# Four gate-up units side by side, modulation sums by transposes, other down groups, tiles moved by 32 bytes: a two-layer hybrid step on one core

## The chip, the cores and the metric

The kernel runs on one core of a Trainium2 chip. The metric is the time of one execution on the device in microseconds (us). Engines carry the profile's names: PE is TensorE's matmul, PEld its weight load, DVE is VectorE, ACT ScalarE, POOL GpSimd, SP SyncE, which issues the DMAs.

## The reference

One inference step of two layers with width 1024 over 1024 latent tokens and 256 prompt tokens. Cut to what matters here:

```
mod_p = silu(c_ctx) @ w_mod[l] + b_mod[l]          # six vectors of 1024 for prompt tokens
mod_s = silu(c) @ w_mod[l] + b_mod[l]              # the same for latent tokens
...
hp = modulate(rms_norm(xp, norm_mix[l]), sh1_p, sc1_p)
hs = modulate(rms_norm(xs, norm_mix[l]), sh1_s, sc1_s)
... # layer 0: neighbourhood attention and pooling; layer 1: windowed attention
xp = xp + g1_p * op
xs = xs + g1_s * os_
hp = modulate(rms_norm(xp, norm_ffn[l]), sh2_p, sc2_p)
hs = modulate(rms_norm(xs, norm_ffn[l]), sh2_s, sc2_s)
xp = xp + g2_p * swiglu(hp, w_gate_up[l], w_down[l])
xs = xs + g2_s * swiglu(hs, w_gate_up[l], w_down[l])
...
y_prompt = rms_norm(xp, norm_final)
y_sample = rms_norm(xs, norm_final)
```

`swiglu` is (silu(h @ gate) * (h @ up)) @ down, with 2816 hidden columns (22 units of 128).

## The kernel before, in words

**Numbers in parts.** Every large product is a sum of three matmuls: operands are split into a high and a low part, and high weights meet both parts of the activations, low weights the high part (`dense_k`, L302 to L308; `prod`, L851 to L858; `mix`, L967 to L976). ScalarE makes the high part, VectorE or GpSimd the low one.

**Blocks.** Tokens come in three blocks: ti = 0 and 1 are latent tokens (512 each), ti = 2 is the prompt (256). A matmul has 512 or 256 columns.

**Weights.** `Weights` (L220) keeps a fixed list of units in the order in which TensorE takes them. A unit is loaded, in some cases summed by GpSimd (L270 to L274), split by ScalarE (L279) and VectorE (L281) into one of four `whl` buffers. `done(i)` starts the split of unit i + 4.

**FFN.** `out_proj` (L794) ends a mixer: two groups of four output rows, each over ti = 0, 1, 2; L809 adds the result to the residual x, the second group feeds the norm. Then `ffn` (L835) runs 22 units. For the latent blocks a unit is seven products of 12 matmuls in Strassen's manner (Q11, Q21, T2, T1, T3, Q22, T4), which need sums of the two latent blocks as operands (T1 to T4) and sums of gate and up weights (units G, A, B, U of the weight list). For the prompt it is a gate and an up product of 24 matmuls with 256 columns. `front(i)` issues Q11 and Q21, `prompt_gate(i)` the prompt's gate, `back(i)` the rest. At the start the order is front(0), front(1), both prompt gates, back(0), back(1).

**Operands of the FFN.** `norm_parts` (L471) returns tasks that turn x into operands: `scaled` (L478, reads the norm factor in PSUM), `high` (L481), `low` (L484), and for the latent blocks `first` to `fourth` (L511 to L532), whose low parts GpSimd makes (L496). They stand in a background list; `bg.step(n)` runs up to n of them as the matmuls are recorded, and `bg.need(key)` all that carry a key. Every engine keeps the recorded order.

**Modulation ahead of time.** `Mod` (L346) computes modulation vectors for later use on VectorE: for each of 20 blocks j of 512 columns, 8 steps of two accumulations (L375, L377) into two tiles, one per condition; then `sum` (L384): matmuls with ones over the 128 partitions and a copy by ScalarE (L389); then `finish` (L391): four transposes (L394) and `mod_done` (L320). That is 10 steps per block. `md.step()` calls stand in the input projection of layer 0 (60 of them), in its output projection and in its FFN; `md.all()` runs what is left at the end of a stage. Layer 1 has none.

**Down.** The hidden units are spilled to DRAM (`hd`) and come back in groups of 4, 4, 4, 4, 4 and 2 chunks (`GROUPS`, L788). `down(q)` mixes group q into x for 8 row blocks m; L976 adds to x, which was itself reloaded (`load_x`). The last group goes block by block and feeds the next norm (`norm_tasks`, L437: L446 and L450), whose tasks run between mixes and in the next input projection; after layer 1 it is the final norm (L426, L435, L1586).

**Attention** of layer 0 starts with score matmuls (L612) and a first pass on VectorE (L626).

Of the kernel before, what the change touches and what calls it, by code (L numbers as in the profile page):

```python
# [87 lines left out]
def lay_out(x):  # L88
# [21 lines left out]
        [wd[l, :, m:m + 2, 4 * q:4 * q + 4].reshape(128, 1024) for q in range(5) for m in range(0, 8, 2)]  # L110
        + [wd[l, :, m:m + 4, 20:22].reshape(128, 1024) for m in (0, 4)], 0).reshape(NHC, 128, 1024)
# [12 lines left out]
def hybrid_step(ctx: ExitStack, tc: tile.TileContext, I: dict, O: list):  # L124
# [22 lines left out]
    padr.tile([128, 24], F32, name="pad")  # L147
# [72 lines left out]
    class Weights:  # L220
# [3 lines left out]
        def __init__(self, jobs, on_pool=()):  # L224
# [4 lines left out]
            for i, j in enumerate(jobs):  # L229
# [3 lines left out]
                elif i == pairs[0]:  # L233
# [237 lines left out]
    def norm_parts(nm, x, l, ti, A, g2):  # L471
# [34 lines left out]
        t1, (xp, ts, t3, t4) = {}, g2[1:]  # L506
# [3 lines left out]

        def first(c):  # L511
            dve.tensor_tensor(x[0][c], xc(c), x[0][c], op=OP.subtract)
            two(A[1].half(0)[:, 0, c], A[1].half(0)[:, 1, c], x[0][c])

        def second(c):
            t = t1[c] = npool.tile([128, 512], F32, name="s2", bufs=3)
            dve.scalar_tensor_tensor(t, x[0][c], mvec(l, 3, c + 4, 0), xc(c + 4), op0=OP.subtract, op1=OP.subtract)
            two(ts[:, 0, c], ts[:, 1, c], t)

        def third(c):  # L520
            t, u = t1.pop(c), npool.tile([128, 512], F32, name="s2", bufs=3)
            dve.scalar_tensor_tensor(u, x[0][c + 4], mvec(l, 3, c + 4, 0), t, op0=OP.add, op1=OP.add)
            t4[c] = instead(0, c)
            two(*t4[c], u)

        def fourth(c):
            high(c + 4)
            low(c + 4)
# [884 lines left out]
    A = A1  # L1413
# [220 lines left out]
```

## Time and profile before

| what | value |
|---|---|
| runs | 3156.12, 3156.30, 3158.57 us (median 3156.30) |
| the profiled execution's own time | 3151.51 us, span 3149.7 us |
| mean granted clock of TensorE | 0.97 |
| busy: TensorE, VectorE, ScalarE, GpSimd | 94%, 58%, 35%, 28% |
| FFN of layer 0 in the profile | gate-up until 1263.3 us, down until 1582.4 us |
| FFN of layer 1 in the profile | gate-up until 2821.0 us, down until 3131.2 us |

A wait is counted for the engine that stands idle, with the engine and the line that ended it. The granted clock is a share of full speed: at 1.00 TensorE ran at 2.4 GHz all the time, at 0.50 at 1.2 GHz.

### The profile page before, as it was taken

Reading aid. Unit: us, or ns where it says so; the run is one execution under the profiler, and the core shown is the slowest. Engines: PE = TensorE matmul, PEld = TensorE weight load, DVE = VectorE, ACT = ScalarE, POOL = GpSimd, SP = SyncE. Lnnn points to the kernel's source line nnn. Section 1 sums busy time; section 2 is a strip of 40 time slices with the busy share of each in tenths; the row PEclk is TensorE's granted clock in tenths of the full one; section 3 lists DMA queues with packets and bytes.
Section 4 is the critical chain, followed back from the end, with each engine's and each line's share of the span. In section 5 each row is a group of like instructions: output and inputs, shape, how many; then the busy total and the mean of one; then the engine's idle time right before and its main releaser. Section 6 shows DMA issues by size and latency. Waiting matters only on the chain.

```text
span 3149.7 us, 46220 instructions
## 1 busy us (share of the span) xinstructions
PE 2957.1 (94%) x18074; PEld 2476.1 (79%) x18074; DVE 1825.9 (58%) x2945; ACT 1101.2 (35%) x2108; POOL 882.5 (28%) x742
## 2 busy tenths in 40 slices
PE   6999999978989989999979999999799999999998
PEld 4877777766878778788868777778688888888886
DVE  5665665466767675455555588872655555543335
ACT  4233772332333232100133477771433333320002
POOL 0341551353323332000222244440543333320002
PEclk9999999989999999999989999999899999999999
DMA  6467555213334334743324411004022223355231
GB/s 249 145 215 252 144 145 154 75 54 107 124 121 124 104 130 148 278 162 135 128 73 143 169 58 47 35 20 143 34 98 97 91 91 104 102 204 200 107 134 67
DMA packets 184330, 394.55 MB, mean 125 GB/s; under 512 B 32176, under 2 KB 69424, under 8 KB 177840
## 3 DMA queue, kind: packets, MB, share of 16 engines
q1 hardware_dynamic: 180656, 385.34, 35.6%
q0 software_dynamic: 3456, 6.26, 0.8%
q8 instruction: 143, 2.34, 0.3%
q14 instruction: 75, 0.61, 0.1%
HBM read 274.32 MB, written 118.23 MB: 125 GB/s over the span
## 4 chain that ended last, share of the span: by engine, by line
PE 70%; DVE 11%; ACT 6%; POOL 5%; issue 4%; DMA 3%; SPq 0%; DVEq 0%; ACTq 0%; POOLq 0%
PE psd L307 7%; PE psd L306 7%; PE psd L308 7%; PE psd L972 6%; PE psd L973 6%; PE psd L974 6%; PE psd L856 5%; PE ps_t L664 5%; PE psd L858 5%; PE psd L857 5%; PE ps_o L680 4%; PE ps_s L612 4%; DVE nacc L377 3%; ACT whl L279 2%; DVE whl L281 2%
## 5 line engine op out<-in xcount | busy, mean ns | idle before, releaser
L307 PE MATMUL psd<-A,whl 128*128 128x256 f32 (+1 forms) x1760 | 584.6, 332 | 42.0 <-DVE A L484 23.3
L306 PE MATMUL psd<-A,whl 128*128 128x256 f32 (+1 forms) x1760 | 587.8, 334 | 16.1 <-ACT A L481 7.8
L308 PE MATMUL psd<-A,whl 128*128 128x256 f32 (+1 forms) x1760 | 580.1, 330 | 1.6 <-DVE whl L281 1.6
L307 PEld LDWEIGHTS psd<-A,whl 128*128 128x128 f32 x1760 | 338.3, 192 | 86.8 <-DVE A L484 28.0
L279 ACT ACTIVATE whl<-wraw 128x1024 fp32r<-128x1024 f32 x178 | 187.2, 1055 | 597.6 <-PE psd L974 476.3
L972 PE MATMUL psd<-A,whl 128*128 128x512 f32 (+1 forms) x1056 | 376.9, 357 | 8.5 <-DMA A<-hd 8.5
L306 PEld LDWEIGHTS psd<-A,whl 128*128 128x128 f32 x1760 | 338.9, 193 | 58.1 <-ACT A L481 8.7
L973 PE MATMUL psd<-A,whl 128*128 128x512 f32 (+1 forms) x1056 | 375.2, 355 | 0.0
L974 PE MATMUL psd<-A,whl 128*128 128x512 f32 (+1 forms) x1056 | 374.9, 355 | 0.0
L308 PEld LDWEIGHTS psd<-A,whl 128*128 128x128 f32 x1760 | 342.6, 195 | 30.7 <-DVE whl L281 2.9
L976 DVE SCALAR_TENSOR_TENSOR x<-psd,modv,x 128x512 f32<-128x512 f32 (+1 forms) x288 | 189.1, 661 | 297.3 <-PE psd L974 277.8
L281 DVE TENSOR_TENSOR whl<-wraw,whl 128x1024 fp32r<-128x1024 f32 x174 | 236.4, 1361 | 157.8 <-ACT whl L279 157.4
L856 PE MATMUL psd<-A,whl 128*128 128x512 f32 x704 | 278.9, 396 | 0.0
L857 PE MATMUL psd<-A,whl 128*128 128x512 f32 x704 | 276.6, 393 | 0.0
L858 PE MATMUL psd<-A,whl 128*128 128x512 f32 x704 | 276.6, 393 | 0.0
L654 POOL TENSOR_SCALAR sP<-sP,sm 128x896 f32<-128x896 f32 (+2 forms) x206 | 179.3, 875 | 245.7 <-DVE sm L647 116.8
L420 POOL TENSOR_TENSOR nacc<-nacc,s 128x512 f32<-128x512 f32 (+1 forms) x84 | 96.4, 1147 | 507.7 <-ACT s L419 504.6
L972 PEld LDWEIGHTS psd<-A,whl 128*128 128x128 f32 x1056 | 200.4, 190 | 39.9 <-issue 12.5
L974 PEld LDWEIGHTS psd<-A,whl 128*128 128x128 f32 x1056 | 201.6, 191 | 28.0
L377 DVE SCALAR_TENSOR_TENSOR nacc<-wmod,cond_raw,nacc 128x512 f32<-128x512 f32 x280 | 211.0, 804 | 19.6 <-DMA wmod<-in_w_mod_dram 19.6
L973 PEld LDWEIGHTS psd<-A,whl 128*128 128x128 f32 x1056 | 200.3, 190 | 27.3
L664 PE MATMUL ps_t<-ident,sP 128*128 128x128 f32 x1408 | 205.8, 284 | 7.8 <-POOL sP L654 2.9
(199 smaller groups left out, 5151.6 us busy)
## 6 DMA issues: line engine op xcount, KB each, us to landing
hd<-x SPq DMA_DIRECT2D x88, 512.0 KB, 3.1
wmod<-in_w_mod_dram SPq DMA_DIRECT2D x160, 256.0 KB, 3.1
A<-hd SPq DMA_DIRECT2D x20, 2048.0 KB, 11.3
wraw<-in_w_gu_dram SPq DMA_DIRECT2D x60, 512.0 KB, 3.7
wraw<-in_w_down_dram SPq DMA_DIRECT2D x44, 512.0 KB, 3.6
wrawx<-in_w_gu_dram SPq DMA_DIRECT2D x28, 512.0 KB, 3.6
A<-hd SPq DMA_DIRECT2D x14, 1024.0 KB, 14.5
hd<-ph SPq DMA_DIRECT2D x44, 256.0 KB, 3.3
```

The costliest lines, as they stand in the source:

```text
L281: eng.tensor_tensor(h[:, 1], src, h[:, 0].bitcast(F32), op=OP.subtract)
L306: pe.matmul(ps[:, :n], wh, A[ti].part(0, k), start=(k == 0), stop=False)
L307: pe.matmul(ps[:, :n], wh, A[ti].part(1, k), start=False, stop=False)
L308: pe.matmul(ps[:, :n], wl, A[ti].part(0, k), start=False, stop=(k == 7))
L377: dve.scalar_tensor_tensor(a, t, cond_raw[:, k, c:c + 1], a, op0=OP.mult, op1=OP.add)
L664: pe.transpose(pt[:, 128 * (i - lo):128 * (i - lo) + 128], P[u][:, 128 * j:128 * j + 128], ident)
L856: pe.matmul(pt, wh, t(0, c), start=(c == 0), stop=False)
L857: pe.matmul(pt, wh, t(1, c), start=False, stop=False)
L858: pe.matmul(pt, wl, t(0, c), start=False, stop=(c == 3))
L972: pe.matmul(pt[:, :n], wh, t[:, 0, k], start=(k == 0), stop=False)
L973: pe.matmul(pt[:, :n], wh, t[:, 1, k], start=False, stop=False)
L974: pe.matmul(pt[:, :n], wl, t[:, 0, k], start=False, stop=(k == nk - 1))
```

## The change

It has four parts.

1. *FFN start.* A function `begin` takes the place of front, prompt gate and back of units 0 and 1: Q11 and Q21 of both, both prompt gates, Q22 of unit 0, T1 of both, T2 of both, then the rest. The tasks of `norm_parts` are put in the order Q22's operand, first, second, third, fourth, each with a key of its own; two low parts of T2 and of T4 go to VectorE. In `out_proj` five background tasks run per step (4 and 1 for the prompt) where it was three, and two latent tasks stand ahead of each prompt task. Four weights of the last group are released earlier, and the weight list begins G, G, A, B, A, B, U, U.
2. *Modulation sums.* The ones-matmul and ScalarE's copy go. After the last accumulation come two empty steps, then for each of the two tiles a step with four transposes of the tile and a reduction on VectorE (L402 of the changed kernel), then `mod_done`: 13 steps per block. Gate-up units have six `mstep` calls where they had four.
3. *Down groups* are 2, 4, 4, 4, 4, 4. In the last group two background tasks run per mix, and the empty places ahead of the norm's tasks are (1, 1) for every block.
4. *Addresses.* 32 of the 96 bytes of padding on the right side move to the left side of the on-chip memory, so the large tiles start 32 bytes further.

The diff, cut to its core:

```diff
-        + [wd[l, :, m:m + 4, 20:22].reshape(128, 1024) for m in (0, 4)], 0).reshape(NHC, 128, 1024)
+        [wd[l, :, m:m + 4, 0:2].reshape(128, 1024) for m in (0, 4)]
+        + [wd[l, :, m:m + 2, q:q + 4].reshape(128, 1024) for q in range(2, NHC, 4) for m in range(0, 8, 2)], 0).reshape(NHC, 128, 1024)
...
-    padr.tile([128, 24], F32, name="pad")
+    padr.tile([128, 16], F32, name="pad")
+    consts.tile([128, 8], F32, name="padl")
...
-                self.pending = [lambda: self.sum(self.acc), lambda: self.finish(l, j)]
+                acc, v = self.acc, npool.tile([128, 32], F32, name="mv", bufs=2)[:, 0:8].rearrange("p (b x) -> p b x", x=2)
+                self.pending = [None, None, lambda: self.sum(acc[0], v, 0), lambda: self.sum(acc[1], v, 1),
+                                lambda: mod_done(l, j, v)]
...
-        def sum(self, acc):
-            ps = ps_tile()
-            for c in range(2):
-                pe.matmul(ps[64 * c:64 * c + 64, :], ones, acc[c], start=True, stop=True, tile_position=(0, 64 * c))
-            self.s = acc[0]
-            act.activation(self.s, ps, AF.Copy)
-        def finish(self, l, j):
+        def sum(self, acc, v, c):
             pt = ps_tile()
             for b in range(4):
-                pe.transpose(pt[:, 128 * b:128 * b + 128], self.s[:, 128 * b:128 * b + 128], ident)
-            mod_done(l, j, pt.rearrange("p (b c i) -> p b c i", b=4, c=2)[:, :, :, 0])
+                pe.transpose(pt[:, 128 * b:128 * b + 128], acc[:, 128 * b:128 * b + 128], ident)
+            dve.tensor_reduce(v[:, :, c], pt.rearrange("p (b i) -> p b i", b=4), axis=AX.X, op=OP.add)
...
         def second(c):
+            dve.scalar_tensor_tensor(x[0][c], x[0][c], mvec(l, 3, c + 4, 0), xc(c + 4), op0=OP.subtract, op1=OP.subtract)
+            two(ts[:, 0, c], ts[:, 1, c], x[0][c], pool if c % 2 else dve)
...
+        def fourth(c):
+            t = temp(x[0][c + 4], mvec(l, 3, c + 4, 0), x[0][c], OP.add, OP.add)
             t4[c] = instead(0, c)
+            two(*t4[c], t, pool if c % 2 else dve)
+        return [("Q22", 0, f) for f in tasks] + [(k, 0, lambda c=c, f=f: f(c)) for k, f in (
+            ("Q22", q22), ("T1", first), ("T2", second), ("T3", third), ("T4", fourth)) for c in range(4)]
...
-    GROUPS = [4, 4, 4, 4, 4, 2]
+    GROUPS = [2, 4, 4, 4, 4, 4]
...
-                    bg.step(3)
+                    bg.step((5, 5, 4 if j else 1)[ti])
...
-                            bg.q += t[:1] + q[:1]
-                            q, t = q[1:], t[1:]
+                            bg.q += t[:2] + q[:1]
+                            q, t = q[1:], t[2:]
...
+        def begin():
+            for i in range(2):
+                front(i, S[i])
+            for i in range(2):
+                prompt_gate(i, S[i])
+            ws = W.take(4)
+            wa, wb = ws[0::2], ws[1::2]
+            W.st = xp.tile([128, 1024], F32, name="x2_0")
+            bg.need("Q22")
+            m3 = [prod(wb[0][1], 512, "Q22")]
+            bg.need("T1")
+            m5 = [prod(wa[i][1], 512, "T1") for i in range(2)]
+            bg.need("T2")
+            for i in range(2):
+                m = prod(wa[i][1], 0, "T2")
...
+            bg.need("T4")
...
-                    mix(q, m, ti, ws[m // 4][1], 256 * (m % 4), nm)
-                    bg.step(1)
+                    mix(q, m, ti, ws[m // 2][1], 512 * (m % 2), nm)
+                    bg.step(2)
...
-        front(0, S[0])
-        front(1, S[1])
-        prompt_gate(0, S[0])
-        prompt_gate(1, S[1])
-        back(0, S[0])
-        back(1, S[1])
+        begin()
...
-        norm_tasks(nm, lambda c: xt[ti][c], 1, 0, ti, A1, ((8, 1), (6, 1), (0, 1))[ti])
+        norm_tasks(nm, lambda c: xt[ti][c], 1, 0, ti, A1, (1, 1))
```

**What moves, first place: VectorE at the FFN start**, around the last operands of the prompt (A21 is the prompt's second half, x2_1 its residual, s2 a temporary of a latent combination). The order before:

```order
L517 SCALAR_TENSOR_TENSOR s2_6259<-x0_3_4702,modv_93,x1_7_4714 128x512
L478 SCALAR_TENSOR_TENSOR x2_1_4716<-x2_1_4716,moda_94,psd_6164 128x256
L484 SCALAR_TENSOR_TENSOR A21_6243<-x2_1_4716,modv_93,A21_6243 128x256
L522 SCALAR_TENSOR_TENSOR s2_6269<-x0_7_4706,modv_93,s2_6259 128x512
L478 SCALAR_TENSOR_TENSOR x2_1_4716<-x2_1_4716,moda_94,psd_6164 128x256
L484 SCALAR_TENSOR_TENSOR A21_6243<-x2_1_4716,modv_93,A21_6243 128x256
L484 SCALAR_TENSOR_TENSOR A11_6080<-x1_7_4714,modv_93,A11_6080 128x512
L530 SCALAR_TENSOR_TENSOR s2_6283<-x1_7_4714,shd_95,x1_3_4710 128x512
L478 SCALAR_TENSOR_TENSOR x2_1_4716<-x2_1_4716,moda_94,psd_6164 128x256
L484 SCALAR_TENSOR_TENSOR A21_6243<-x2_1_4716,modv_93,A21_6243 128x256 x2
L281 TENSOR_TENSOR whl_6304<-x2_0_6301,whl_6304 128x1024
```

The last low parts of the prompt (L484 to A21) stand behind every latent combination: L517 and L522 are those of T2 and T4, L530 that of T3, and directly ahead of the low half of unit 0's A weights (L281). The order after, with L485, L491, L517 and L503 for what were L478, L484, the combinations and the low parts of `two`:

```order
L485 SCALAR_TENSOR_TENSOR x2_1_4741<-x2_1_4741,moda_95,psd_6204 128x256
L491 SCALAR_TENSOR_TENSOR A21_6253<-x2_1_4741,modv_94,A21_6253 128x256
L485 SCALAR_TENSOR_TENSOR x2_1_4741<-x2_1_4741,moda_95,psd_6204 128x256
L491 SCALAR_TENSOR_TENSOR A21_6253<-x2_1_4741,modv_94,A21_6253 128x256
L517 SCALAR_TENSOR_TENSOR s2_6287<-x0_4_4728,modv_94,x0_0_4724 128x512
L503 TENSOR_TENSOR x0_4_6290<-s2_6287,x0_0_6289 128x512
L491 SCALAR_TENSOR_TENSOR A21_6253<-x2_1_4741,modv_94,A21_6253 128x256
L517 SCALAR_TENSOR_TENSOR s2_6294<-x0_5_4729,modv_94,x0_1_4725 128x512
L517 SCALAR_TENSOR_TENSOR s2_6300<-x0_6_4730,modv_94,x0_2_4726 128x512
L503 TENSOR_TENSOR x0_6_6303<-s2_6300,x0_2_6302 128x512
L283 TENSOR_TENSOR whl_6335<-st_5768,whl_6335 128x1024
```

The last A21 now stands ahead of three of the four T4 combinations (L517 from x0_5 on), and low parts of T4 (L503) are VectorE's own.

**Second place: the end of the first input projection.** TensorE before, with the last dense matmuls, the transposes of the last sum and the first scores:

```order
L306 MATMUL psd_2507<-A21_687,whl_2066 128x256
L307 MATMUL psd_2507<-A21_687,whl_2066 128x256
L308 MATMUL psd_2507<-A21_687,whl_2066 128x256
L394 MATMUL psd_2532<-ident_72,nacc_2326 128x128 x4
L612 MATMUL ps_s_2570<-Ka_2125,Qa_2203 128x512
L612 MATMUL ps_s_2571<-Ka_2125,Qa_2203 128x512
```

TensorE after:

```order
L308 MATMUL psd_2479<-A21_688,whl_2041 128x256
L309 MATMUL psd_2479<-A21_688,whl_2041 128x256
L310 MATMUL psd_2479<-A21_688,whl_2041 128x256
L401 MATMUL psd_2513<-ident_73,nacc_2327 128x128 x4
L401 MATMUL psd_2519<-ident_73,nacc_2328 128x128 x4
L401 MATMUL psd_2554<-ident_73,nacc_2527 128x128 x4
L401 MATMUL psd_2560<-ident_73,nacc_2528 128x128 x4
L620 MATMUL ps_s_2595<-Ka_2098,Qa_2176 128x512
L620 MATMUL ps_s_2596<-Ka_2098,Qa_2176 128x512
```

Two sums, each of two rows of four transposes, now stand between the last dense matmul and the first score. VectorE in the same place before, with the accumulations of the modulation (L377) among the evacuations of the projection (L757):

```order
L377 SCALAR_TENSOR_TENSOR nacc<-wmod,cond_raw,nacc 128x512 x4
L757 TENSOR_TENSOR stg<-psd,stg 128x512
L377 SCALAR_TENSOR_TENSOR nacc<-wmod,cond_raw,nacc 128x512 x4
L757 TENSOR_TENSOR stg<-s_2465,stg 128x512
L757 TENSOR_TENSOR stg<-psd,stg 128x256
L323 TENSOR_TENSOR modv<-psd,bmod 128x8
L328 SCALAR_TENSOR_TENSOR moda<-modv,norms 128x8
L759 SCALAR_TENSOR_TENSOR stg<-psd,stg 128x256
L626 ISA sP,sm<-ps_s,gb_2560 128x896
```

And after (L387 and L389 are the accumulations, L765 and L767 the evacuations, L402 the reductions, L634 the first pass over the scores):

```order
L765 TENSOR_TENSOR stg<-psd,stg 128x256
L389 SCALAR_TENSOR_TENSOR nacc<-wmod,cond_raw,nacc 128x512 x2
L767 SCALAR_TENSOR_TENSOR stg<-psd,stg 128x256
L402 TENSOR_REDUCE mv<-psd 128x4 x2
L325 TENSOR_TENSOR modv<-mv,bmod 128x8
L330 SCALAR_TENSOR_TENSOR moda<-modv,norms 128x8
L387 TENSOR_SCALAR nacc<-wmod,cond_raw 128x512 x2
L389 SCALAR_TENSOR_TENSOR nacc<-wmod,cond_raw,nacc 128x512 x14
L402 TENSOR_REDUCE mv<-psd 128x4 x2
L325 TENSOR_TENSOR modv<-mv,bmod 128x8
L330 SCALAR_TENSOR_TENSOR moda<-modv,norms 128x8
L634 ISA sP,sm<-ps_s,gb_2585 128x896
```

One whole block, sixteen accumulations, stands behind the last evacuation (L767) and ahead of the last two reductions and the scores.

## Rows read from the trace of the kernel before

**Rows 1.** The page's first part: busy time, share of the span, instructions.
```profile
PE 2957.1 (94%) x18074; PEld 2476.1 (79%) x18074; DVE 1825.9 (58%) x2945; ACT 1101.2 (35%) x2108; POOL 882.5 (28%) x742
```

**Rows 2.** Waits of TensorE: line, engine and line that ended it, us, times, longest.
```profile
PE psd L387 <- DVE nacc L377: 41.1, 7, 12.9
...
PE psd L307 <- DVE A L484: 23.3, 16, 3.0
...
PE psd L307 <- DVE A L450: 18.3, 11, 5.0
...
PE psd L972 <- DMA A<-hd: 8.5, 2, 4.6
```

**Rows 3.** Table by stretch: length, busy of PE, PEld, DVE, ACT, POOL, clock, DMA.
```profile
603.60:666.40 62.80, 40.83 (x212) 34.65 (x211) 47.88 (x63) 28.33 (x52) 37.47 (x29) 0.76 0.07 21
666.40:1263.30 596.90, 550.99 (x2871) 464.00 (x2869) 382.64 (x460) 180.82 (x265) 185.97 (x129) 0.96 0.37 123
1263.30:1582.40 319.10, 314.45 (x1632) 267.34 (x1633) 160.83 (x241) 39.97 (x51) 25.34 (x20) 0.98 0.47 172
1580.00:1670.00 90.00, 71.01 (x335) 56.10 (x335) 49.41 (x77) 31.16 (x54) 16.60 (x13) 0.89 0.20 71
2294.10:2821.00 526.90, 526.90 (x2812) 456.86 (x2811) 281.69 (x323) 178.41 (x257) 191.79 (x129) 1.00 0.31 108
2821.00:3131.20 310.20, 305.56 (x1599) 263.42 (x1597) 122.00 (x171) 34.30 (x43) 19.57 (x16) 0.99 0.34 131
3131.20:3149.70 18.50, 3.00 (x20) 2.34 (x18) 12.67 (x26) 2.23 (x7) 3.62 (x5) 0.65 0.67 242
```

**Rows 4.** Timeline of TensorE at 750 to 767: start, us, line, [idle before <- what ended it].
```profile
749.79 0.39 PE L858 MATMUL psd<-A,whl 128*128 128x512 f32 x1
...
751.15 0.39 PE L858 MATMUL psd<-A,whl 128*128 128x512 f32 x1
...
764.40 2.63 PE L387 MATMUL psd<-nacc,ones 128*64 128x512 f32 x4 [12.87 <-DVE nacc L377]
```

**Rows 5.** Timeline of TensorE at four other places.
```profile
130.10 1.08 PE L387 MATMUL psd<-nacc,ones 128*64 128x512 f32 x4
...
299.83 0.28 PE L307 MATMUL psd<-A,whl 128*128 128x256 f32 x1
...
301.71 0.28 PE L308 MATMUL psd<-A,whl 128*128 128x256 f32 x1
...
842.17 0.66 PE L394 MATMUL psd<-ident,nacc 128*128 128x128 f32 x4 [1.54 <-ACT nacc L389]
...
903.11 2.63 PE L387 MATMUL psd<-nacc,ones 128*64 128x512 f32 x4 [8.13 <-DVE nacc L377]
```

**Rows 6.** Groups of VectorE by form: the reductions from PSUM, whole span.
```profile
L620 DVE TENSOR_REDUCE sm<-ps_s 128x2 f32<-128x512 f32 x24 | 16.0, 680 | 1.6 <-PE ps_s L612 1.6
```

**Rows 7.** Timeline of VectorE at 280 to 306.
```profile
286.54 2.74 DVE L377 SCALAR_TENSOR_TENSOR nacc<-wmod,cond_raw,nacc 128x512 f32<-128x512 f32 x4
```

**Rows 8.** Groups of VectorE and GpSimd by form, 603.6 to 666.4.
```profile
L484 DVE SCALAR_TENSOR_TENSOR A<-x,modv,A 128x512 fp32r<-128x512 f32 x8 | 9.4, 1177 | 4.1 <-ACT A L481 4.1
...
L478 DVE SCALAR_TENSOR_TENSOR x<-x,moda,psd 128x512 f32<-128x512 f32 x11 | 7.6, 738 | 0.0
...
L496 POOL TENSOR_TENSOR x<-s,x 128x512 fp32r<-128x512 f32 x8 | 10.9, 1358 | 9.6 <-ACT x L495 9.6
```

**Rows 9.** Groups of VectorE by form, 1582 to 1605.
```profile
L450 DVE SCALAR_TENSOR_TENSOR A<-s,modv,A 128x512 fp32r<-128x512 f32 x8 | 11.5, 1438 | 0.1
```

**Rows 10.** Timeline of VectorE at 2820 to 2845.
```profile
2835.10 1.41 DVE L976 SCALAR_TENSOR_TENSOR x<-psd,modv,x 128x512 f32<-128x512 f32 x2 [5.33 <-DMA x<-xr]
...
2840.35 2.24 DVE L976 SCALAR_TENSOR_TENSOR x<-psd,modv,x 128x256 f32<-128x256 f32 x4 [3.85 <-DMA x<-xr]
```

**Rows 11.** Timeline of TensorE at 395 to 405: score matmuls of L612.
```profile
397.44 1.49 PE L612 MATMUL ps_s<-Ka,Qa 64*128 64x512 f32 x12
...
402.37 1.51 PE L612 MATMUL ps_s<-Ka,Qa 64*128 64x512 f32 x12
```

More of the change, by code (lines that the diff above doesn't have):

```diff
@@ L515, in second @@
         def second(c):
[L516 to L518 removed]
+            dve.scalar_tensor_tensor(x[0][c], x[0][c], mvec(l, 3, c + 4, 0), xc(c + 4), op0=OP.subtract, op1=OP.subtract)
+            two(ts[:, 0, c], ts[:, 1, c], x[0][c], pool if c % 2 else dve)
         def third(c):
[L521 to L540 removed]
+            t = temp(xc(c + 4), shd[:, l, c:c + 1], xc(c), OP.add, OP.subtract)
+            t3[c] = instead(1, c)
+            two(*t3[c], t)
+        def fourth(c):
+            t = temp(x[0][c + 4], mvec(l, 3, c + 4, 0), x[0][c], OP.add, OP.add)
+            t4[c] = instead(0, c)
+            two(*t4[c], t, pool if c % 2 else dve)
+        return [("Q22", 0, f) for f in tasks] + [(k, 0, lambda c=c, f=f: f(c)) for k, f in (
+            ("Q22", q22), ("T1", first), ("T2", second), ("T3", third), ("T4", fourth)) for c in range(4)]
     class Unit:
@@ L844, in ffn, with mstep @@
         H, now = {}, [0]
-        def mstep(n=1):
-            for _ in range(n):
-                if md is not None and now[0] > 1:
-                    md.step()
+        def mstep():
+            if md is not None and now[0] > 1:
+                md.step()
         def prod(w, off, name):
@@ L859, in prod, with place @@
             return pt
+        def place(i, ti):
+            return hd[(i + 2) // 4][ti][:, :, i if i < 2 else (i + 2) % 4, :]
         def spill(i, ti, src):
@@ L884, in front @@
             act.activation(a, m, AF.Copy)
-            bg.step(5)
+            bg.step(6 if i else 2)
             mstep()
@@ L899, in prompt_gate, with up_prompt @@
             act.activation(sg[:, 0:256], pg[:, 0:256], AF.Silu)
-            if i == 0:
-                W.st = xp.tile([128, 1024], F32, name="x2_0")
             W.done(wi)
-            bg.step(5)
+            bg.step(2)
+        def up_prompt(i, s, w):
+            pu, sg = ps_tile(), s["sg"]
+            dense(pu, w, A, 2)
+            dve.tensor_tensor(sg[:, 0:256], sg[:, 0:256], pu[:, 0:256], op=OP.mult)
+            h = gq.tile([128, 2, 256], F32R, name="ph", bufs=1)
+            hi_lo(h[:, 0], h[:, 1], sg[:, 0:256])
+            sp.dma_start(place(i, 2), h.bitcast(F32))
@@ new lines, in c21, with c12 @@
+        def c21(i, s, w, v):
+            m = prod(w, 512, "T4")
+            dve.tensor_tensor(v, v, m, op=OP.add)
+            dve.tensor_tensor(s["c"], s["c"], v, op=OP.mult)
+            spill(i, 0, s["c"])
+        def c12(i, a, z):
+            act.activation(a, a, AF.Silu)
+            dve.tensor_tensor(a, a, z, op=OP.mult)
+            spill(i, 1, a)
+        def begin():
[13 more added lines that the diff above has]
+                m = prod(wa[i][1], 0, "T2")
+                dve.tensor_tensor(S[i]["a"], S[i]["a"], m, op=OP.add)
+                if i == 0:
+                    W.done(wa[0][0])
+            bg.need("T4")
+            for i in range(2):
+                a = S[i]["a"]
+                if i == 1:
+                    m3.append(prod(wb[1][1], 512, "Q22"))
+                m = prod(wb[i][1], 0, "T3")
+                v, z = (npool.tile([128, 512], F32, name="s2", bufs=3) for _ in range(2))
+                dve.tensor_tensor(v, a, m, op=OP.add)
+                W.done(wb[i][0])
+                if i == 0:
+                    W.done(wa[1][0])
+                dve.tensor_tensor(a, a, m5[i], op=OP.add)
+                dve.tensor_tensor(z, v, m5[i], op=OP.add)
+                dve.tensor_tensor(a, a, m3[i], op=OP.add)
+                c12(i, a, z)
+                wi, w = W.take(1)[0]
+                up_prompt(i, S[i], w)
+                c21(i, S[i], w, v)
+                W.done(wi)
@@ L916, in back @@
             W.done(wi)
-            wi, w = W.take(1)[0]
+            mstep()
+            (wi, w), (ui, uw) = W.take(2 if last else 1) + ([] if last else [(None, None)])
+            if last:
+                up_prompt(i, s, uw)
+                load_h(0, 2)
             m = prod(w, 0, "T3")
@@ L960, in down @@
                 for m in range(8):
-                    mix(q, m, ti, ws[m // 4][1], 256 * (m % 4), nm)
-                    bg.step(1)
+                    mix(q, m, ti, ws[m // 2][1], 512 * (m % 2), nm)
+                    bg.step(2)
+                    if ti == 2 and m % 2:
+                        W.done(ws[m // 2][0])
                 tail(ti, nm)
-            for wi, _ in ws:
-                W.done(wi)
         def mix(q, m, ti, w, off, nm):
```

84 lines of the change are left out of this document (41 added, 43 removed).

## The prediction

> **What bounds the kernel now.** I read the page's shares first: TensorE is busy for 94% of a span of 3149.7 us [rows 1]. Only idle TensorE time and time at its lower clock can be won, so the second view was the list of what TensorE waits for [rows 2], and the third a table of stretches [rows 3]. The reader should see in it that the loss sits in few places. A stretch without loss gives the pace: six 512-column matmuls start 1.36 us apart in all, 0.2267 us each [rows 4]; 256 columns take 0.1175 us (sixteen in 1.88 us) [rows 5].
>
> Five places are open.
> - *FFN start.* From 603.6 to 666.4 the program holds 96 + 48 matmuls of 256 columns and 48 of 512, so 16.9 + 10.9 = 27.8 us; it takes 62.8 [rows 3]. The two prompt gates wait for L484 on VectorE, which is busy 47.9 of the 62.8 us. Layer 1 repeats it.
> - *Modulation sums.* Gate-up of layer 0, with 8 sums, takes 596.9 us; the same units in layer 1, without sums, take 526.9 and keep TensorE full [rows 3]. That is 70.0 us, 8.75 a sum. In [rows 4] TensorE's queue stands 12.87 us at a sum until VectorE's accumulation is done; the granted clock of 0.96 [rows 3] says that some of the work behind such gaps runs at the lower level.
> - *Between the layers.* 1580 to 1670 has 19.0 us of idle TensorE and a granted clock of 0.89: 19.0 + 0.11 x 90 = 29 us, waiting for L450 [rows 2, 3].
> - *The end.* After the last mixing 18.5 us are left [rows 3].
> - *The start of each down phase*, 4 to 5 us of waiting for the reloaded hidden block [rows 2].
>
> **The change, term by term**, against the profiled execution (3151.51 us; the median of the runs shown is 4.8 above it).
>
> *Sums in gate-up: -53.* Sums by transposes need no ones-matmul and no ScalarE copy. A sum was one ones block of 1.08 us, a wait for the copy (1.54 us at 842) and four transposes of 0.66 together [rows 5]. It becomes twice four transposes, at most 2 x 0.66; their ends overlap what follows, so I take 1.2 us. The deciding part is its place: a sum stood right behind the last accumulation in TensorE's queue; now two empty steps go between, so it stands three products (3 x 2.72 = 8.2 us, with a prompt block of 2.8 us 11) later. At 903.1 TensorE had stood there for 8.13 us [rows 5], so most of that wait goes. With six steps per unit and 13 per column block, ten blocks pass in gate-up: 10 x 1.2 = 12 us, plus 0 to 1.2 us of wait each; I take 5 in all. 70 - 17 = 53. Bounds: 40 (two waits of 6 us and their clock stay) and 60. What hides the new VectorE work: two reductions of at most 0.68 us (the row of a reduction from PSUM) [rows 6] a block, and two blocks more; 382.6 + 2 x 11 + 14 = 419 us in 544, 77% of its time.
>
> *Sums elsewhere: -7.5.* Down of layer 0 is 8.9 us longer than that of layer 1 [rows 3] for four sums; two remain, -5. In the output projection two sums with small waits: -2.5.
>
> *End of the first input projection: +8.* Here the change costs. There are 60 step slots and six blocks need 78 steps, so 18 run after the last dense: the order shows sixteen accumulations in a row and all transposes ahead of the first attention score. Four accumulations took 2.73 us [rows 7], so sixteen take 10.9; with reductions and transposes 12.5, and some 3 us of lower clock behind the gap. Of the 41.1 us at sums [rows 2] the long ones lie in gate-up and some 3.3 here; with them, six sums at 1.2 instead of 1.08 + 0.66 give back 3.3 + 6 x 0.54 = 6.5, say 7. Bounds -5 (attention hides the delay later) and +14.
>
> *FFN start: -20.* Before, a latent task and a prompt task alternate, so the prompt's last operand, which both gates wait for, comes last of all. Now three of the fourth combinations stand behind it and are needed only after ten products of other operands, and out_proj takes five background tasks a step. Against that, four low weight halves come into VectorE's stretch. Counted to the prompt's last operand, the order holds 56 VectorE instructions; at the mean durations of this stretch they are 46 us, no less than now: gain 0. At their shortest durations they are 33 us: gain 22 per layer. What lies between is who shares with GpSimd: L484, both inputs in SBUF, takes 1.18 us; L478, which reads PSUM, 0.74 [rows 8]; four of sixteen GpSimd subtractions of 1.36 us or more [rows 8] leave the stretch, and four weight sums enter. I add what cannot overlap if such instructions exclude one another: 22 us of GpSimd and 21 us of VectorE at shortest durations, 43, where the same count for the kernel before is 49 and took 57 of the 62.8 us. By that ratio the prompt is ready 7 us earlier, and 3 more come from the earlier start: -10 per layer, bounds 0 and -22.
> The Trainium skill, "SBUF — State Buffer", section "Who interferes with whom", says that a VectorE instruction with two SBUF inputs and a GpSimd instruction that reads SBUF lock each other out of a shared port pair for a whole instruction. The trace agrees in kind (1.18 against 0.74 us). By that rule alone, all 43 us in series and nothing else waiting, the term would be -28 for both layers instead of -20.
>
> *Between the layers: -26.* Down's last group now has 4 chunks: a mix of 512 columns is 12 matmuls, 2.72 us, where it was 1.36. Latent block 0's norm is covered by the mixing of blocks 1 and 2, 8 x 1.36 + 8 x 0.70 = 16.5 us before, 33 now. The norm costs VectorE eight times a product that reads PSUM (0.74, as L478 [rows 8]) and a low part of 1.44 [rows 9], 17.4 us. So the 29 us go, less 3 for bubbles between norm matmuls. Bounds -18 and -29.
>
> *The end: -4.5.* Of these 18.5 us VectorE works 12.7 [rows 3]. Block 1's final scaling (eight instructions that read PSUM, like the 0.74 of L478 [rows 8]: 5.9 us) now fits into 8 x 12 x 0.1175 = 11.3 us of mixing of the prompt, where half of that held its norm's sums only. What stays is the prompt's own norm, scaling and the outputs. Bounds -2 and -7.
>
> *Start of down: +3.* With two chunks the first group needs half the block, so the 4.6 us wait goes. Late next are the residual tiles: VectorE's first evacuation waited for them until 2835.1 and 2840.4 [rows 10], 14 and 19 us into the phase. A first mix is now 1.36 us and eight PSUM banks are full after some 9 us, so TensorE stalls there instead, 7 to 8.5 us against nearly 7 with its clock. +1.5 per layer, bounds -3 and +4.
>
> *Tiles moved by 32 bytes: 0.* No row shows a dense matmul at such an address. The nearest rows are the score matmuls, whose key windows start at 0 or 32 bytes: twelve take 1.49 to 1.51 us [rows 11], and the six that read windows differ by at most 0.02 / 6 = 3.3 ns. Times 12,144 dense matmuls (7568 of 512 columns and 4576 of 256, counted in the program) that is 40 us as the far end; most of that difference would come from twelve window rows per matmul, a contiguous row crosses one boundary, so I take the lower end.
>
> Sum: -53 - 5 - 2.5 + 8 - 20 - 26 - 4.5 + 3 = -100. 3151.5 - 100 = 3051.5 profiled, **3056 us** as a median.
>
> **Rivals.**
> 1. *VectorE becomes the pace of layer 0's gate-up.* It is busy 382.6 of 596.9 us there against 281.7 of 526.9 without modulation [rows 3], works in queue order and waits for ScalarE's high halves; each latent product needs its evacuation before the next combination. If each of twenty units slips by 1.5 us (my estimate, 1 to 2), 30 us of the 53 come back: 3086. For: it was 8 us behind at 903 [rows 5]. Against: it catches up while TensorE waits only at sums. It decides when VectorE's work and the waits it cannot hide exceed the new unit, 544 / 22 = 24.7 us; its work alone is 419 / 22 = 19.0.
> 2. *The FFN start is freed altogether*, -22 per layer: 3032. For: durations at their shortest when GpSimd is quiet. Against: GpSimd is not.
> 3. *The FFN start gains nothing*, the gates still waiting for the prompt's operand at contended durations: 3076. The change then does not do there what it says.
> 4. *The 32 bytes slow every matmul* (slower). 0.2267 us for 512 columns is 17 clocks of 2.4 GHz per 16 columns, that is per 64 bytes. If each 64 bytes straddled a boundary and took one clock more, 512 columns would cost 13.3 ns and 256 columns 6.7 ns more: 7568 x 13.3 + 4576 x 6.7 ns = 131 us, 3187. It outweighs the rest from about 9 ns per matmul (100 us over 12,144, a little more for the wide). Against it: the 3.3 ns at most of [rows 11].
>
> **How the numbers follow.** Forecast 0.58, VectorE's pace 0.13, FFN start free 0.13, FFN start unmoved 0.12, slower matmuls 0.04. Independent bounds of the forecast (13 in gate-up, 20 at the FFN starts, 8 and 13 at the projections) add in square to about 30. Low end 3022 holds rival 2 with some to spare, high end 3094 rivals 1 and 3. A measurement of this kernel can tell 0.2%, 6.3 us, from no change. Only rival 4 or a heap of far ends reaches that: faster 0.95, same 0.01, slower 0.04.
>
> **What would show it.** In the new profile: gate-up of layer 0 near 544 us with waits at the transposes under 2 us each (53 right); longer with waits spread over product lines (rival 1). No stretch between the layers with a clock under 0.95; a gap of 12 us ahead of the first score; prompt gates of unit 0 about 10 us earlier relative to the last output-projection dense; TensorE waiting for VectorE's residual adds 10 us into each down phase. Layer 1's units at 23.95 us (526.9 / 22) as now; 25 or more would prove rival 4. I am wrong if the time is under 3022, which needs a gain in places I counted as full, or over 3094.

## The result and the profile after

The changed kernel takes 3138.85 us (median of 4 runs, 3136.18 to 3142.91) against 3156.21: a ratio of 0.9944, interval 0.9927 to 0.9962. That is 17 us less instead of the 100 forecast: a real gain, as the interval stays under 1, but the time lies above the range. The profiled execution took 3142.91 us, with a span of 3141.1. It is the slowest of its four, and the profiled one of before (3151.51) was faster than all four there, so the stages below add up to only 8.6 us less than those of before.

Lengths of the stages, from TensorE's timelines of both kernels, in us:

| stage | before | after | difference | forecast |
|---|---|---|---|---|
| start to the first score | 302.7 | 316.2 | +13.5 | +8 |
| attention, output projection up to its last latent dense | 300.8 | 302.4 | +1.6 | -2.5 |
| FFN start to the end of unit 1, layer 0 | 95.7 | 102.3 | +6.6 | -10 |
| units 2 to 21, layer 0 | 564.8 | 517.3 | -47.5 | -53 |
| down, layer 0 | 318.4 | 347.5 | +29.1 | -3.5 |
| input projection, layer 1 | 199.1 | 179.4 | -19.7 | -26 |
| attention, output projection, layer 1 | 450.0 | 449.9 | -0.1 | 0 |
| FFN start, layer 1 | 95.6 | 106.1 | +10.5 | -10 |
| units 2 to 21, layer 1 | 493.9 | 493.9 | 0 | 0 |
| down, layer 1, and the end | 328.7 | 326.1 | -2.6 | -3 |

The table by stretch of the kernel after, in the order of [rows 3]: FFN start to the end of the second prompt gate, the rest of gate-up, down, the start of the next projection, then gate-up, down and the end in layer 1:

```profile
618.60:688.10 69.50, 38.14 (x212) 33.38 (x211) 45.72 (x66) 29.17 (x51) 29.04 (x24) 0.75 0.06 19
688.10:1238.20 550.10, 540.16 (x2882) 467.12 (x2881) 413.98 (x502) 172.34 (x254) 185.13 (x124) 0.99 0.41 133
1238.20:1585.80 347.60, 316.70 (x1634) 271.64 (x1634) 169.51 (x248) 45.57 (x60) 23.69 (x19) 0.95 0.42 156
1585.80:1655.40 69.60, 60.64 (x316) 51.83 (x315) 27.72 (x52) 22.54 (x41) 17.91 (x11) 0.93 0.35 112
2288.10:2815.00 526.90, 526.90 (x2810) 456.72 (x2810) 278.76 (x327) 176.80 (x255) 183.56 (x123) 1.00 0.31 103
2815.00:3128.60 313.60, 306.79 (x1609) 263.91 (x1607) 129.43 (x183) 36.44 (x47) 21.74 (x19) 0.99 0.37 143
3128.60:3141.10 12.50, 1.76 (x7) 1.22 (x6) 5.36 (x13) 1.09 (x3) 1.45 (x2) 0.62 0.48 168
```

Gate-up of layer 0 has come from 596.9 to 550.1 us, with a granted clock of 0.99; the end from 18.5 to 12.5. But in down of layer 0 TensorE now stands for 31 us, and at the FFN start for 31 again, where it was 22. The list of TensorE's waits says for whom:

```profile
PE psd L433 <- DVE nacc L427: 55.6, 5, 19.1
PE psd L401 <- DVE nacc L389: 30.9, 6, 12.5
PE psd L1032 <- DVE x L1036: 30.8, 6, 12.6
PE psd L433 <- POOL nacc L427: 19.2, 5, 9.0
...
PE psd L309 <- DVE A L491: 9.5, 7, 2.3
```

L401 are the new sums, L433 the sums of squares of a norm (13.2 of its 55.6 us lie at the start of the program, where it was 13.5), L1032 a mix whose PSUM bank VectorE (L1036) has not emptied. Waits for low parts have shrunk from 23.3 [rows 2] to 9.5 (L309); L433 and L1032 have taken their place. Three places follow.

**Down, layer 0.** VectorE's timeline in the kernel *before* has a wait that no list of TensorE's waits shows:

```profile
1302.41 1.42 DVE L377 SCALAR_TENSOR_TENSOR nacc<-wmod,cond_raw,nacc 128x512 f32<-128x512 f32 x2 [11.51 <-DMA wmod<-in_w_mod_dram]
```

It stood 11.5 us at an accumulation whose w_mod tile came late, and TensorE went on mixing into free PSUM banks, 2.72 us a mix. After, VectorE first, then TensorE:

```profile
1280.85 1.42 DVE L389 SCALAR_TENSOR_TENSOR nacc<-st,cond_raw,nacc 128x512 f32<-128x512 f32 x2 [13.24 <-DMA st<-in_w_mod_dram]
```

```profile
1258.99 0.58 PE L1032 MATMUL psd<-A,whl 128*128 128x256 f32 x1 [11.02 <-DVE x L1036]
...
1282.98 0.79 PE L1032 MATMUL psd<-A,whl 128*128 128x512 f32 x1 [12.60 <-DVE x L1036]
```

The same wait, 13.2 us, now stops TensorE for 12.6, because mixes of 1.36 us fill the banks in half the time.

**The last group of the same phase.** VectorE's timeline after, while block 1 is mixed (L1036 evacuates a mix; L453 and L457 are the norm of block 0):

```profile
1553.53 0.74 DVE L1036 SCALAR_TENSOR_TENSOR x<-psd,modv,x 128x512 f32<-128x512 f32 x1
1554.20 0.73 DVE L453 SCALAR_TENSOR_TENSOR s<-x,moda,psd 128x512 f32<-128x512 f32 x1
1554.85 0.74 DVE L457 SCALAR_TENSOR_TENSOR A<-s,modv,A 128x512 fp32r<-128x512 f32 x1
1556.77 0.75 DVE L453 SCALAR_TENSOR_TENSOR s<-x,moda,psd 128x512 f32<-128x512 f32 x1 [1.18 <-POOL nacc L427]
1557.44 0.75 DVE L457 SCALAR_TENSOR_TENSOR A<-s,modv,A 128x512 fp32r<-128x512 f32 x1
1558.10 0.74 DVE L1036 SCALAR_TENSOR_TENSOR x<-psd,modv,x 128x512 f32<-128x512 f32 x1
```

One evacuation comes 4.57 us after the other, where TensorE needs 2.72 for a mix. So the sums of squares are late, and TensorE's timeline shows it behind block 1 and behind the prompt:

```profile
1571.52 1.86 PE L433 MATMUL psd<-ones,nacc 128*128 128x1 f32 x8 [6.40 <-POOL nacc L427]
...
1600.33 1.01 PE L433 MATMUL psd<-ones,nacc 128*128 128x1 f32 x4 [8.96 <-POOL nacc L427]
```

**FFN start.** VectorE, then TensorE, in layer 0:

```profile
642.87 1.22 DVE L283 TENSOR_TENSOR whl<-st,whl 128x1024 fp32r<-128x1024 f32 x1 [5.06 <-ACT whl L281]
...
650.66 0.47 DVE L817 SCALAR_TENSOR_TENSOR x<-psd,modv,x 128x256 f32<-128x256 f32 x1
...
653.80 1.47 DVE L427 TENSOR_TENSOR nacc<-nacc,s 128x256 f32<-128x256 f32 x1 [2.67 <-POOL nacc L427]
657.51 1.23 DVE L283 TENSOR_TENSOR whl<-wraw,whl 128x1024 fp32r<-128x1024 f32 x1 [2.24 <-ACT whl L281]
```

```profile
655.33 1.02 PE L433 MATMUL psd<-ones,nacc 128*128 128x1 f32 x4 [19.12 <-DVE nacc L427]
```

VectorE stands 5.06 us for the summed A weights of unit 0, then works 6.6 us on latent operands, and only then comes to the prompt's last evacuation (L817), which the sum of squares needs. TensorE's queue, with Q21 next, stands at that sum.

### The profile page after: what moved, and what is told of

The parts are those of the page before. It is cut to its first block, busy times and chain, and to the rows that moved or that the text cites. A ratio compares the mean times of both kernels' runs of the same rounds, so it can differ in the third digit from the quotient of the medians.

```text
span 3141.1 us, 46254 instructions
## 1 busy us (share of the span) xinstructions
PE 2939.9 (94%) x18074; PEld 2489.3 (79%) x18074; DVE 1853.1 (59%) x3007; ACT 1090.4 (35%) x2084; POOL 852.4 (27%) x720
## 3 DMA queue, kind: packets, MB, share of 16 engines
q8 instruction: 143, 2.34, 0.3%
## 4 chain that ended last, share of the span: by engine, by line
PE 74%; DVE 10%; ACT 5%; POOL 4%; issue 3%; DMA 3%; SPq 0%; POOLq 0%; DVEq 0%; ACTq 0%
PE psd L309 8%; PE psd L308 8%; PE psd L310 8%; PE psd L863 6%; PE psd L864 6%; PE psd L865 6%; PE psd L1032 6%; PE psd L1033 6%; PE psd L1034 6%; PE ps_t L672 5%; PE ps_o L688 4%; PE ps_s L620 4%; DVE nacc L389 2%; ACT whl L281 1%; ACT sT L677 1%
## 5 line engine op out<-in xcount | busy, mean ns | idle before, releaser
L309 PE MATMUL psd<-A,whl 128*128 128x256 f32 (+1 forms) x1760 | 580.9, 330 | 9.9 <-DVE A L491 9.5
L281 ACT ACTIVATE whl<-wraw 128x1024 fp32r<-128x1024 f32 x178 | 187.5, 1055 | 665.0 <-PE psd L1034 479.6
L1032 PE MATMUL psd<-A,whl 128*128 128x512 f32 (+1 forms) x1056 | 378.6, 359 | 30.9 <-DVE x L1036 30.8
L309 PEld LDWEIGHTS psd<-A,whl 128*128 128x128 f32 x1760 | 338.4, 192 | 45.5 <-DVE A L491 11.0
L1036 DVE SCALAR_TENSOR_TENSOR x<-psd,modv,x 128x512 f32<-128x512 f32 (+1 forms) x288 | 187.7, 661 | 300.8 <-PE psd L1034 283.8
L427 POOL TENSOR_TENSOR nacc<-nacc,s 128x512 f32<-128x512 f32 (+1 forms) x78 | 89.4, 1147 | 837.0 <-ACT s L426 833.7
L1032 PEld LDWEIGHTS psd<-A,whl 128*128 128x128 f32 x1056 | 201.0, 190 | 61.2 <-DVE x L1036 33.4
L672 PEld LDWEIGHTS ps_t<-ident,sP 128*128 128x128 f32 x1408 | 153.3, 143 | 56.4 <-issue 24.9
```

Source lines behind the costliest of these rows:

```text
L281: act.activation(h[:, 0], src, AF.Copy)
L309: pe.matmul(ps[:, :n], wh, A[ti].part(1, k), start=False, stop=False)
L672: pe.transpose(pt[:, 128 * (i - lo):128 * (i - lo) + 128], P[u][:, 128 * j:128 * j + 128], ident)
L1032: pe.matmul(pt[:, :n], wh, t[:, 0, k], start=(k == 0), stop=False)
```

## The experiments

Times are medians. A ratio is to the kernel before, run again beside each group of experiments (medians 3153.3 to 3156.6 us).

**Modulation out of the first down group** (`elif ti == 0:` became `elif ti == 0 and q > 0:` ahead of `mstep()` in `mix`).

> The changed kernel with no modulation steps during the first down group of layer 0. Theory: TensorE's 12.6 us wait at 1283 in the changed kernel is VectorE standing 13.2 us at an accumulation whose w_mod half is on its way behind 5 MB of hidden blocks, with the evacuations queued behind it; without that accumulation the wait goes and the kernel is 13 to 17 us faster than the changed one (3122 to 3126). Rival: the residual tiles alone are late and set both waits (11.0 and 12.6); then nothing moves, 3136 to 3142.

3123.03 us, ratio 0.9895 (0.9880 to 0.9909): the theory. Down of layer 0 is 15.6 us shorter; the first wait, for the residual tiles, stays at 10.8.

**First down group block by block, block 1 first**, on top of that:

```diff
+            if q == 0:
+                ws = W.take(2)
+                for ti in (1, 0, 2):
+                    for m in range(8):
+                        mix(q, m, ti, ws[m // 4][1], 256 * (m % 4), None)
...
```

> The changed kernel without modulation in the first down group (3123) and with the first group mixed block by block, block 1 first, whose residual tiles are loaded earlier than those of block 0. Theory: the wait of 10.8 us in layer 0 and of 5.9 in layer 1 is the residual of block 0 on its way; 8 mixes of 1.36 us of block 1 cover it: 3105 to 3112. Rival: VectorE is held by the last unit's spill and by loads that are late for all blocks, and less than 5 us come of it.

3114.30 (0.9870, 0.9853 to 0.9887): between the two. In layer 1 the wait for residual tiles (6.4 us in the first run, 5.9 in the changed kernel) is gone, and 6.6 us with it. In layer 0 only 3.5 us are won; a wait of 4.3 for VectorE stays.

**One background task per mix** in layer 0's last group (`bg.step(2)` became `bg.step(2 if l else 1)`), on top of the first run.

> The changed kernel without modulation in the first down group (as in the run before, 3123) and with one background task per mix instead of two in the last group of layer 0. Theory: with two tasks VectorE needs some 4.6 us for each mix of 2.72, so the sums of block 1's and the prompt's norm come 6.7 and 9.0 us late for TensorE; with one task it keeps pace and 8 to 13 us of it go: 3110 to 3116. Rival: the tasks not run under the mixes are waited for in the next input projection, and the time is 3120 to 3128.

3111.23 (0.9859, 0.9841 to 0.9878): the theory; down is 10.1 us shorter than in the first run and the projection behind it 2.7.

**The sums alone** on the kernel before (the new `sum`, two empty steps, two more `mstep`).

> The kernel before with the new modulation sums and the two more steps per unit alone. Theory (the gain of the change is this part, the rest gives it back): gate-up of layer 0 about 47 us shorter, the first input projection 13 us longer, the other stages as before: 3116 to 3126. Rival: the new sums need the other parts too, and gate-up keeps waits of several us at each block: 3135 or more.

3116.58 (0.9879, 0.9860 to 0.9899): the theory. One part of four gives 39 us, more than twice the whole change.

**The old FFN start** in the changed kernel.

> The changed kernel with the FFN start of before (task order, weight order, release of weights, units 0 and 1 one after the other); sums, down groups and addresses stay changed. Theory: the new start costs 6.8 us in layer 0 and 10.5 in layer 1, so this kernel is 15 to 19 us faster than the changed one: 3119 to 3125. Rival: the loss at the start follows from the down groups or addresses, and the time stays at 3136 to 3142.

3125.12 (0.9904, 0.9888 to 0.9921): the theory, at its edge. This edit also gives the last squares of each norm back to GpSimd. The starts take 96.1 and 95.3 us, as before the change.

**Why the new start is slower.** First the last norm sums on GpSimd (`nms[ti].feed(xc)`), and the late release (`if ti == 2 and (g == 0 or j < 2):`); it concerns two weights, not four as "The change" has it:

> The changed kernel with the last two squares of each norm in the output projection summed by GpSimd, as before the change. Theory F (place of the last sum): VectorE's queue with the operand tasks ahead of that sum makes the 19.1 us wait for the prompt's norm; on GpSimd the wait falls below 9 us in both layers, 3116 to 3124 in all. Rival W (early weights): the wait comes from VectorE standing at the low half of the A weights, with the last evacuation of the prompt behind it; then the 19.1 us stay within 3 us and the time is 3134 to 3143.

> The changed kernel with the weights of the last two output rows released as late as before the change, so that the A and B weights of the FFN are not built among the prompt's evacuations. Theory W (early weights): VectorE no longer stands 5 us at the A weights and GpSimd is free for the sums of squares; the 19.1 us wait falls to under 9 in both layers, 3116 to 3126. Rival F: the wait keeps 16 us or more and the time is 3134 to 3145, or longer because the weights now come late.

3144.31 and 3138.40. Theory F fell: the wait is 18.2 us on GpSimd too, and the time a little above the range of its rival. Theory W was half right: the wait fell to 11.8, but TensorE then stood 4.6 us for a weight and longer at the gates, and the starts are 1.4 and 5.0 us shorter, with next to nothing won in all. Then the order of the tasks (`bg.step((5, 5, 1)[ti])`), and Q22's operand with the low part behind the next scaling:

> The changed kernel with one background task per step for the prompt's part of the output projection instead of four. Theory O (order of tasks): the 19.1 us wait for the prompt's norm comes from latent tasks that stand on VectorE ahead of the prompt's evacuations, whose squares GpSimd and ScalarE need; here that wait falls below 8 us in both layers, and 6 to 16 us are won in all: 3123 to 3133. Rival S (sum of work): VectorE's work up to the first products of sums sets the end in any order; the wait falls but turns up at the prompt gates or at T1 and T2, and the time stays within 4 us, 3135 to 3142.

> The run before this one with the four tasks for Q22's operand written so that the low part of one follows the scaling of the next, instead of scaling, high and low part of one task in a row. Theory: VectorE waited 0.79 us for ScalarE in each of four tasks; 2 to 4 us less per layer, 4 to 8 in all against the run before this one. Rival: that time is idle anyway, since VectorE waits elsewhere for ScalarE or GpSimd; under 2 us in all.

3135.31 and 3137.84. The wait fell to 5.8, as theory O said, and the time hardly did: rival S, and the rival in the second too. The starts of the second are 97.1 and 96.4 us, level with the old ones. But in layer 0 TensorE then stands longer at the first new sum of gate-up, after the change and here:

```profile
770.30 1.11 PE L401 MATMUL psd<-ident,nacc 128*128 128x128 f32 x4 [5.34 <-DVE nacc L389]
```

```profile
767.03 1.12 PE L401 MATMUL psd<-ident,nacc 128*128 128x128 f32 x4 [10.19 <-DVE nacc L389]
```

Units 2 to 21 of layer 0 take 5.8 us longer, about what the start had won there. In layer 1, which has no sums, nearly 10 us stay won up to the end of gate-up; why the median shows so little of them is open (both down phases are about 3 us longer in this profile). Next the low halves of the four summed weights on GpSimd, without and with the prompt's tasks first (units 10 to 13 added to `Weights`' `on_pool` in both layers):

> The changed kernel with the low halves of the four summed weights of units 0 and 1 made by GpSimd instead of VectorE, in both layers. Theory H: VectorE's queue stands 5.1, 2.2, 3.6 and 5.7 us at these four instructions, until GpSimd has summed and ScalarE rounded the weights, with evacuations and operands behind it; without them the 19.1 us wait falls by 5 or more and 8 to 18 us are won over both layers: 3121 to 3131. Rival S: the work of the three engines in series sets the end of the stretch in any order, GpSimd's longer instruction takes the place of the stand, and the time stays in 3134 to 3143.

> The same with one background task per step for the prompt (3135 without the move to GpSimd). Theory H: with the prompt's evacuations first and VectorE not standing at the summed weights, both relieve one another: 3112 to 3126. Rival S: 3130 to 3140, the waits turning up at the prompt gates or at T1 to T4.

3134.84 and 3132.11: the rival again. In the first VectorE no longer stands at the weight, but 5.02 us one link further, at an operand's low part: in ScalarE's queue the operand's high part (L488) stands behind the rounding of the weight (L281), which waits for GpSimd's sum. That low part then takes 2.32 us beside GpSimd's 2.34, where those without such work beside them took 0.75 after the change. The prompt's wait is still 18.6 us.

```profile
637.34 1.06 ACT L281 ACTIVATE whl<-st 128x1024 fp32r<-128x1024 f32 x1 [3.46 <-POOL st L273]
638.30 0.71 ACT L488 ACTIVATE A<-x,modv 128x512 fp32r<-128x512 f32 x1
638.47 2.34 POOL L283 TENSOR_TENSOR whl<-st,whl 128x1024 fp32r<-128x1024 f32 x1 [1.17 <-ACT whl L281]
639.04 2.32 DVE L491 SCALAR_TENSOR_TENSOR A<-x,modv,A 128x512 fp32r<-128x512 f32 x1 [5.02 <-ACT A L488]
...
650.39 1.01 PE L433 MATMUL psd<-ones,nacc 128*128 128x1 f32 x4 [18.62 <-DVE nacc L427]
```

Last the early release on the old start, and the sums taken out (`elif kind in "AB" and self.ns in (10, 11, 12, 13): pass` ahead of `elif kind == "A":`; 10, 11, 13, 14 in the kernel before):

> The changed kernel with the old FFN start (3125) but the early release of the last two output weights kept, so that the sums A and B of unit 0 are built during the prompt's part of the output projection. Theory H: VectorE stands at their low halves ahead of the prompt's evacuations and 6 to 15 us of the loss come back: 3131 to 3140. Rival: the release is harmless and the loss lies in the order of the new start alone: 3122 to 3128.

> The changed kernel without GpSimd's sums for the four summed weights of units 0 and 1 in both layers (the gate weights are split in their place, so these products use other weights). Theory P (price of the sums in the stretch): the new start needs all four before its sixth product, so their chain GpSimd, ScalarE, VectorE lies in the stretch in which GpSimd also makes the operands' low parts; without the sums 8 to 15 us per layer go: 3109 to 3123. Rival: the operands alone set the end of the stretch, and less than 4 us per layer come: 3131 or more.

> The kernel before without the same sums (again with other weights in these products). Theory P: the old start builds them when TensorE has the products of the first operands to do, they lie beside its work, and under 3 us per layer come: 3150 to 3157. Rival: they cost as much as in the new start, 3140 or less.

The early release on the old start costs more than expected: 3146.55 against 3125.12, starts of 107.1 us in both layers instead of 96.1 and 95.3. Without the sums the changed kernel takes 3128.91, 10 us less, between theory and rival, and its starts 99.2 and 96.1; the kernel before takes 3152.21 without them, within its own spread. So the summed weights are a main part of the loss: 3.1 us of layer 0's start and 10.0 of layer 1's, while at the old start, which builds them later, they cost nothing that shows. No order of the new start came under the 96.1 and 95.3 us of the old one; the best are level with it.

**More modulation slots in the first input projection** (a step ahead of every dense, ti = 2 included, and two for ti = 0: 84 slots for 60):

> The changed kernel with 84 instead of 60 step slots for modulation in the first input projection, so that nothing is left to run behind its last dense. Theory: the 15.4 us that TensorE spends at the last transposes ahead of the first score shrink to under 3, and as attention follows at its own pace the whole comes out 10 to 13 us faster, 3126 to 3129. Rival: VectorE falls behind inside the projection, or attention was slack, and less than 4 us come of it.

3157.06 (1.0011, 1.0001 to 1.0020): the rival, and more than that, 18 us slower than the changed kernel. TensorE now waited 5.7, 3.0 and 8.8 us between 160 and 205, where GpSimd works on the pooling, and the first score comes at 324.9 instead of 316.2.

**All mended**: old start, no modulation in the first group, one task per mix, block 1 first; then also a slot more per dense in the last four groups (`if gi > 2: md.step()`).

> The changed kernel with the old FFN start, no modulation in the first down group, one task per mix in layer 0's last group, and the first down group block by block with block 1 first. Theory: the four losses are separate places, so the gains of the single runs add: 3125 - 16 - 12 - 9 = 3088, within 3083 to 3094. Rival: they share a cover (VectorE or the DMA queue), and less than half of the three further gains comes: 3107 or more.

> The run before this one with one more modulation slot per dense in the last four groups of the first input projection, where GpSimd is quiet, instead of 18 steps behind the last dense. Theory: the gap of 15.4 us ahead of the first score shrinks to under 4 with no new waits over 2 us in the projection: 9 to 12 us less than the run before this one (3076 to 3080 if that gives 3088). Rival, as the run with slots in all groups showed: VectorE falls behind in the projection and the sums wait there; less than 3 us are won or the kernel is slower.

The first takes 3088.84 us, ratio 0.9784 (0.9769 to 0.9798), as the single gains add: 2.2% under the kernel before. What TensorE still waits for in it:

```profile
PE psd L400 <- DVE nacc L388: 31.1, 6, 12.3
PE psd L308 <- DVE A L490: 23.5, 16, 3.0
...
PE psd L432 <- POOL nacc L426: 11.6, 6, 4.2
```

These are the sums, above all the one ahead of the first score, and the old start's gates. The second takes 3083.10 (0.9766, 0.9749 to 0.9782). Its median lies 5.7 us under the first, between theory and rival, but the intervals overlap and its runs go from 3082.94 to 3090.67, so it can't be told from it. In the profiled execution, the slowest of its four, the last wait ahead of the scores is 4.7 us, but another has come:

```profile
178.56 1.12 PE L400 MATMUL psd<-ident,nacc 128*128 128x128 f32 x4 [10.79 <-DVE nacc L388]
...
301.02 1.94 PE L400 MATMUL psd<-ident,nacc 128*128 128x128 f32 x8 [4.74 <-DVE nacc L388]
```

Together they are 15.5 us, where the first run has 3.0 and 12.3, and the first score comes at 315.9 us against 313.1: in this profile the rival.

## Why the prediction was right or wrong

From -100 to -8.6 the stages are 91 us apart: 37 of them lie at the two FFN starts, 33 in down of layer 0.

- **Sums in gate-up, -53: right**, -47.5 in units 2 to 21; two waits over 2 us stay there (5.3 and 3.1). Rival 1, VectorE as the pace, did not come: it is busy 414.0 of 550.1 us, 75%, where 77% was worked out.
- **Sums elsewhere, -7.5: wrong in time**, about 0; in down the saved work is there and hidden. Down of layer 0 before, and in the run with the sums alone:

```profile
1264.00:1582.60 318.60, 313.95 (x1631) 266.74 (x1629) 160.33 (x240) 40.08 (x52) 25.54 (x20) 0.99 0.47 172
```

```profile
1224.70:1544.50 319.80, 308.71 (x1622) 266.16 (x1620) 154.24 (x226) 38.65 (x48) 25.44 (x20) 0.98 0.47 170
```

  TensorE is busy 5.2 us less, as the term says. But its wait for the reloaded hidden block is 10.3 us there, where it was 3.8, and the phase is 1.2 longer. The output projection takes 106.8 us in both: there nothing came.
- **First input projection, +8**: mechanism and place right, 12.5 us of wait ahead of the first score as worked out. +13.5 in this profile; the same code gave +5.4 to +12.8 in other runs.
- **FFN start, -20: wrong**, +17.1; rival 3, no gain there, came nearest, and the loss lies outside both bounds. The failed step is "I add what cannot overlap if such instructions exclude one another", with a ratio to the kernel before. The exclusion did shrink, as far as the low parts with both inputs in SBUF show it (L484 before, 1177 ns [rows 8]; L491 after) by form, 618.6 to 688.1:

```profile
L491 DVE SCALAR_TENSOR_TENSOR A<-x,modv,A 128x512 fp32r<-128x512 f32 x7 | 5.2, 749 | 3.3 <-ACT A L488 3.2
```

  VectorE is busy 45.7 us there, less than the 47.9 before [rows 3]. But the stretch is 69.5 us instead of 62.8: VectorE stands 23.8 us where it stood 14.9. A sum of work doesn't give the length when each link (VectorE, ScalarE, GpSimd, VectorE) stands in a queue behind the others. "Four weight sums enter" was costed as GpSimd's time, and only two of their low halves fall into the stretch. What they cost is their place in the queues: at the old start an early release of unit 0's made it 11 to 12 us longer in each layer, and without them the new one is 3.1 and 10.0 us shorter. VectorE's queue alone is not it, since with the low halves on GpSimd the prompt's wait stayed at 18.6 us. How the rest of layer 0's loss divides stays open. The sentence on the Trainium skill's port rule ("SBUF — State Buffer", section "Who interferes with whom") would have made the term -28: the rule is seen in these rows, and was not what bound.
- **Between the layers, -26: wrong by half.** -19.7 in the projection, but some 10 us came back under the last mixes. I compared 17.4 us of VectorE with 33 us of cover in all; what counts is each mix, two tasks and an evacuation, 4.57 us against 2.72. Behind down the granted clock was 0.93, under the 0.95 that was to be the least.
- **Start of down, +1.5 per layer: wrong in layer 0.** The residual wait was foreseen: 7 to 8.5 us, measured 11.0 and 5.9. The w_mod wait of 11.5 us stood on VectorE's timeline of before, in layer 0; [rows 10] are of layer 1, which has no modulation. Halving the mix halved the cover over every stall of VectorE, and I had only looked for TensorE's.
- **The end, -4.5: right**, -6.0, from 18.5 to 12.5. Down of layer 1 is 3.4 longer where 1.5 was forecast; together -2.6 where -3 was summed.
- **32 bytes, 0: right; rival 4 fell.** TensorE in units 2 to 21 of layer 1, before and after:

```profile
2327.20:2821.00 493.80, 493.80 (x2641) 428.44 (x2640) 264.13 (x304) 167.89 (x243) 178.52 (x120) 1.00 0.31 108
```

```profile
2321.10:2815.00 493.90, 493.90 (x2642) 428.40 (x2641) 260.11 (x305) 166.39 (x242) 173.16 (x116) 1.00 0.31 104
```

## What to carry to other kernels

A list of TensorE's waits shows what is exposed now; before a unit of its work is made smaller, read the own waits of the engine that feeds or empties it in the same stretch: each one longer than the new cover will be exposed. Work put into an engine's queue is costed by what stands behind it there and by its longest link, not by its busy time alone. When parts of a change touch separate places, time each alone: here one of four alone gained 39 us, and the others together gave more than half of it back.

## What the runs showed of the hardware that was not expected

The same code up to the first score took between 308.1 and 316.2 us in the fifteen profiles of kernels that share it (in one, the sums alone, the tiles lie 32 bytes lower), 8 us apart, where units 2 to 21 of layer 1 took 493.8 or 493.9 us in every one. At the FFN start of layer 0 VectorE's low parts of 512 columns, with two inputs in SBUF, fell from 1177 to 749 ns in the mean when GpSimd's work in the stretch went from 37.5 to 29.0 us, with no gain in time.
